# Moving every tile that TensorE reads to a multiple of 512 bytes in SBUF

## The chip, the cores and the metric

The kernel runs on one core of one Trainium2 chip. The metric is the device time of one execution in microseconds. Before the change the median of 3 runs is 1949.47 us (1949.44 to 1951.29).

## What is computed

One layer of a decoder: a gMLP token mixer and a SwiGLU feed-forward part, each followed by a residual and a layer norm, all in float32 on 2048 tokens of 1024 features.

```python
D_MODEL = 1024; SEQ = 2048; GM_CHUNK = 128; GM_GROUPS = 8; FFN_HIDDEN = 2816
mod = silu(c) @ mod_w + mod_b                    # six vectors: sh1, sc1, g1, sh2, sc2, g2
h = x * (1 + sc1) + sh1
u, v = split(gelu(h @ gm_w_in + gm_b_in))
v = layer_norm(v)                                # then 128x128 causal products, group by group
y = (u * (w_masked @ v + b_s)) @ gm_w_out
x = layer_norm(2 ** 0.25 * x + (1 + g1) * y)
h = x * (1 + sc2) + sh2
g, u = split(h @ ffn_w_in)
x = layer_norm(2 ** 0.25 * x + (1 + g2) * ((silu(g) * u) @ ffn_w_out))
```

## The kernel before

Every large product is carried as three products of `float32r` parts: an operand is split by `parts` (L88, L89) into a high part (a cast on ScalarE) and a low part (a subtraction on VectorE), and hi*hi, hi*lo and lo*hi are added up in PSUM. Such a tile (`UNIT`) holds 2 x 512 values of 4 bytes on each of 128 partitions, 4096 bytes a partition. One matmul reads a stationary operand of 128 values (512 bytes a partition, loaded just ahead of it) and a moving operand of 512 values (2048 bytes a partition). There are 7881 of these matmuls.

The mixer runs over 4 blocks of 512 tokens. In each, `token_major` (L192) makes v from `hT` and `wv`, `feature_major` (L209) makes u from `wu` and `hT`, small 128x128 products (L310) do the spatial gate, and `token_major` (L192 again) makes y from `yT` and `wo`. The feed-forward part takes Winograd's form of a 2x2 product, seven products P1 to P7. `ffn_in` (L428) runs over two halves of the tokens, 11 pairs of hidden tiles each, the seven products in the order P1, P2, P5, P6, P7, P4, P3, and gate and up ("g" and "u" in the names) for each; one such product is 12 matmuls. `ffn_out` (L577) takes the products in the order P2, P5, P3, P1, P6, P7, P4; in each step it runs 12 matmuls of the first half of the tokens and then 12 of the second; P4's second half comes last, by itself.

Tiles lie in pools that are stacked from the left end of SBUF upward or from the right end downward (`phase("left", ...)`, `phase("right", ...)`). At the left end come 16384 bytes of scratch for DMAs that GpSimd issues (there are two, L110 and L112), then constants and the small tiles of the norms, up to byte 20032, which is 64 modulo 512. At the right end the pools begin at byte 229344, which is 480 modulo 512. All slots of the large pools are whole multiples of 512 bytes, so that every large tile of the left begins at 64 modulo 512 and every one of the right at 480. The matmuls read them so (from the built program's addresses):

| matmuls | stationary operand | moving operand | count |
|---|---|---|---|
| v, L192 | `hT`, right, 480 | `wv`, left, 64 | 768 |
| u, L209 | `wu`, left, 64 | `hT`, right, 480 | 768 |
| y, L192 | `yT`, left, 64 | `wo`, left, 64 | 768 |
| P1 and P2 of `ffn_in`, L428 | weights, left, 64 | `A11`, `A12`, right, 480 | 1056 |
| the other five of `ffn_in`, L428 | weights, left, 64 | left, 64 | 2640 |
| `ffn_out` without P4, first half, L577 | `alw`, right, 480 | `wd_w`, right, 480 | 792 |
| `ffn_out` without P4, second half, L577 | `alw`, left, 64 | `wd_w`, right, 480 | 792 |
| P4 of `ffn_out`, L577 | `alw`, right (222) or left (75) | `wd_w`, left, 64 | 297 |

So in 3606 matmuls (768 + 768 + 1056 + 792 + 222) the two operands begin at different places modulo 512, and in 4275 at the same.

Of the kernel before, what the change touches and what calls it, by code (L numbers as in the profile page):

```python
# [24 lines left out]

# Winograd's form of the 2x2 product C = A B in seven products:
#   P1 = A11 B11   P2 = A12 B21   P5 = S1 T1   P6 = S2 T2   P3 = S4 B22   P7 = S3 T3   P4 = A22 T4
#   S1 = A21 + A22   S2 = S1 - A11   S3 = A11 - A21   S4 = A12 - S2
#   T1 = B12 - B11   T2 = B22 - T1   T3 = B22 - B12   T4 = B21 - T2
#   C11 = P1 + P2         C12 = P1 + P6 + P5 + P3  # L30
#   C21 = P1 + P6 + P7 + P4   C22 = P1 + P6 + P7 + P5
A_OF = {1: "A11", 2: "A12", 3: "S4", 4: "A22", 5: "S1", 6: "S2", 7: "S3"}
# [4 lines left out]
def gmlp_swiglu_layer(  # L37
# [6 lines left out]
):  # L44
    """One gMLP + SwiGLU layer.

    Every large product is float32 carried as three one-pass products: an operand is the exact
    sum of two float32r parts (12 significant bits each), hi and lo, and hi*hi + hi*lo + lo*hi
    is accumulated in float32. The products of the feed-forward part take Winograd's form.
    """  # L50
    nc = tc.nc
# [4 lines left out]
    dram = ctx.enter_context(tc.tile_pool(name="dram", bufs=1, space=bass.MemoryType.DRAM))  # L56

    ROW, HALF, UNIT = ([P, D], F32), ([P, 512], F32), ([P, 2, 512], F32R)
    cur, n = {}, [0]

    def phase(side, **tags):
        """Open one pool for each tag: tag=(number of slots, shape and type). Close what is returned."""
        st = ExitStack()
        for tag, (bufs, kind) in tags.items():
            n[0] += 1
            p = st.enter_context(tc.tile_pool(name=f"{tag}{n[0]}", bufs=bufs, side=side, reuse_waits="tile"))
            cur[tag] = (p, kind)
        return st
# [16 lines left out]
    def parts(src, name, tag):  # L85
        """[P, 512] float32 as its hi and lo parts."""
        o = new(tag, name, UNIT)
        nc.scalar.copy(out=o[:, 0, :], in_=src)  # L88
        nc.vector.tensor_tensor(out=o[:, 1, :], in0=src, in1=o[:, 0, :].bitcast(F32), op=ALU.subtract)  # L89
        return o  # L90
# [7 lines left out]

    # constants
    ident = const.tile([P, P], F32, name="ident")  # L100
# [5 lines left out]

    # conditioning: mod = silu(c) @ mod_w + mod_b, one column per 128 outputs
    modc = const.tile([P, 48], F32, name="modc")
# [29 lines left out]
    def spread(k, name):  # L138
        """Columns [P, 1] * ND as one row on every partition, by way of DRAM."""
        line = dram.tile([ND, P], F32, name=f"{name}_line")  # L140
        nc.sync.dma_start(out=line.rearrange("d p -> p d"), in_=modc[:, k * ND : (k + 1) * ND])
        t = new("late", name)
        nc.sync.dma_start(out=t, in_=line.rearrange("d p -> (d p)").partition_broadcast(P))
        return t
# [4 lines left out]
    def norm_of(st, name):  # L149
        """Mean and 1 / sqrt(var + EPS)."""  # L150
        mv = small.tile([P, 2], F32, tag="mv", name=f"{name}_mv")
        nc.vector.bn_aggr(out=mv, in_=st)
        ve = small.tile([P, 1], F32, tag="ve", name=f"{name}_ve")
        nc.vector.tensor_scalar(ve, mv[:, 1:2], EPS, None, ALU.add)  # L154
        rs = small.tile([P, 1], F32, tag="rs", name=f"{name}_rs")
        nc.gpsimd.tensor_tensor(out=rs, in0=ve, in1=mhalf, op=ALU.pow)  # L156
        # one Newton step: rs * (1.5 - 0.5 * ve * rs^2)
        nw = small.tile([P, 1], F32, tag="nw", name=f"{name}_nw")
        nc.vector.scalar_tensor_tensor(out=nw, in0=rs, scalar=ve, in1=rs, op0=ALU.mult, op1=ALU.mult)
        nc.vector.tensor_scalar(nw, nw, -0.5, 1.5, ALU.mult, ALU.add)  # L160
        nc.vector.tensor_tensor(out=rs, in0=rs, in1=nw, op=ALU.mult)
        return mv[:, 0:1], rs
# [10 lines left out]
    def ahead(makers, depth=2):  # L173
        """The makers' results in order; each is made `depth` uses before its own."""
        made = [m() for m in makers[:depth]]

        def results():
            for i in range(len(makers)):
                if i + depth < len(makers):
                    made.append(makers[i + depth]())  # L180
                yield made[i]

        return results()

    def token_major(operands, nk, name, between=()):
        """out[t, :] over NT token tiles: sum over k of a_k[:, t].T @ w_k, in all 8 banks."""
        ps = [[bank(f"{name}_ps{t}{h}") for h in range(2)] for t in range(NT)]
        for k, (a, w) in enumerate(operands):
            for t in range(NT):
                for part, wpart in HL:  # L190
                    for h in range(2):
                        nc.tensor.matmul(  # L192
                            ps[t][h],
                            lhsT=a[:, part, t * P : (t + 1) * P],
                            rhs=w[h][:, wpart, :],
                            start=(k == 0 and part == 0 and wpart == 0),
                            stop=(k == nk - 1 and part == 1),
                        )
            for f in between[k :: nk]:
                f()  # L200
        return ps

    def feature_major(w, rhs, name):
        """out[j, tokens] of 128 features: w is [d, (d-tile, j)] in parts."""
        ps = bank(name)
# [13 lines left out]
    x1d = [dram.tile([TB, D], F32, name=f"x1d{b}") for b in range(NB)]  # L219
    # left operands of the feed-forward products, [k, tokens of one half] in float32  # L220
    hop = [[[dram.tile([P, TB], F32, name=f"hop{o}_{k}_{sb}") for sb in range(2)] for k in range(NK)] for o in range(7)]
# [11 lines left out]
    def setup_spatial():  # L233
        # masked w_s, transposed to [s, (g, t)]
        wm = new("bcv", "wm")
# [5 lines left out]
        )  # L241
        # tb[c, (g, t)] = ln_b[c] * sum_s w[t, s] + b_s[g, t]
        lb = new("raw", "lnb_bc")
# [122 lines left out]
    def h2_part(b, i, cols_of, tag):  # L366
        """Transposed, modulated feature tiles i and NK + i; with the second half of a super-block their left operands.

        cols_of(t, q) is token tile t's columns of feature tile i + q * NK.
        """  # L370
        sb = b // 2
# [28 lines left out]
    def a_operands(r0, r1, name):  # L400
        """Raw [k0, (t0, t1)] and [k1, (t0, t1)] -> S1..S4 and the seven left operands in float32."""
        a11, a21, a12, a22 = r0[0], r0[1], r1[0], r1[1]
# [7 lines left out]
    def load_ops(sb, names):  # L410
        def tag_of(n, k):
            """A22, S3 and most of S4 take rows that the mixer leaves."""
            return "late" if n in ("A22", "S3") or (n == "S4" and k > 1) else "ops" + n

        out = {}
        for n in names:
            out[n] = []
            for k in range(NK):
                t = new("h3" if sb else "s" if n in ("S3", "A22") else "hr", f"h2{n}r_{sb}_{k}", HALF)
                nc.sync.dma_start(out=t, in_=hop[A_AT[n]][k][sb])  # L420
                out[n].append(parts(t, f"h2{n}_{sb}_{k}", tag_of(n, k)))
        return out

    def ffn_in(sb, ops, between={}):
# [12 lines left out]
        def weight(fp, pr, gu):  # L437
# [6 lines left out]
            b11, b12, b21, b22 = B[gu]  # L444
            # T1, T2 take the place of B11, T3 of B12, T4 of B21
            if pr == 5:
# [13 lines left out]
        for fp in range(NP):  # L460
            X, Y, Z, c1, u1, u2 = {}, {}, {}, {}, {}, {}
            for pr in order:
# [30 lines left out]
                if (fp, pr) in between:  # L493
                    between[fp, pr]()
            # C11 in c1, C12 in u1, C22 in u2, C21 in X
            for cc in (c1, u2, u1):
# [8 lines left out]
    def residual(b, t, r, cs, st, scaled=False):  # L505
        """r * (1 + g2) + alpha * x1 on half a row, with its sums."""
        xt = new("xr", f"xr{b}_{t}_{cs.start}")[:, : cs.stop - cs.start]
# [10 lines left out]
    def finish(b, t, r, st, e):  # L518
        """Norm and store of one token tile; `e` adds, or none where the wait for it would be the longest."""
        row = b * TB + t * P  # L520
# [15 lines left out]

    # token tile pairs: (sb, p) joins tile p of the first and of the second half of sb
    prs = [(sb, p) for sb in range(2) for p in range(NT)]
# [44 lines left out]
    def ffn_out():  # L583
# [29 lines left out]

        # P3 adds to P5 and P6, P7, P4 to P1 where they accumulate; the last product of the second half
        # comes pair by pair, so that each pair's norm follows at once
        steps = [(pr, k) for pr in (2, 5, 3, 1, 6, 7, 4) for k in range(NP)]
# [153 lines left out]
```

## Time and profile before

| | |
|---|---|
| median of 3 runs | 1949.47 us (1949.44 to 1951.29) |
| profiled execution, first to last instruction (its span) | 1948.5 us; the page gives no other time of it |
| median less span | 1.0 us |
| TensorE busy | 1875.5 us, 96% of the span, 8297 matmul records |
| VectorE, ScalarE, GpSimd busy | 1284.1, 760.2, 716.6 us |
| DMA | 312.77 MB, 161 GB/s on average |

Busy time of TensorE is modelled and overlaps from one matmul to the next, so the pace of the matmuls is not read from it. The pace is read from the chain of work that ended last: a piece "2.72 ... x12" says that 12 matmuls in a row took 2.72 us of that chain. The granted clock of TensorE (PEclk) is in shares of full speed: 1.00 is 2.4 GHz and 0.50 is 1.2 GHz.

### The profile page before, as it was taken

The page shows a single profiled execution, that of the slowest core. Times are in us where ns is not written, and L with a number is a line of the kernel's source. Part 1 is how long each engine was busy: PE and PEld are TensorE (multiplying, and loading weights), DVE is VectorE, ACT ScalarE, POOL GpSimd, SP SyncE. Part 2 cuts the span into 40 slices and gives each one's busy share as a digit, 9 for nine tenths or more (in the row PEclk, how much of TensorE's full clock was granted, in tenths as well). Part 3 has the DMA queues.
Part 4 walks back from the last instruction along what each step waited for, and adds up shares of the span by engine and source line. Part 5 has one row for each costly group of instructions (what it writes and reads, how often), then busy time and mean ns, then how long its engine had stood idle before and what let it go on. Part 6 is the DMA issues. An engine that isn't in the chain of part 4 may idle for free.

```text
span 1948.5 us, 23471 instructions
## 1 busy us (share of the span) xinstructions
PE 1875.5 (96%) x8297; PEld 1532.5 (79%) x8297; DVE 1284.1 (66%) x1855; ACT 760.2 (39%) x1251; POOL 716.6 (37%) x465
## 2 busy tenths in 40 slices
PE   7999999999999999999999999999999999999776
PEld 6787788778888788888887888888888888887655
DVE  8486866786758856555668566556554433476998
ACT  3432552543545434333345333333343443332321
POOL 0000500550402666645544554355431200244834
PEclk9999999999999999999999999999999999999978
DMA  9358546464455444542236323322347644555542
GB/s 355 121 184 304 170 153 229 156 226 155 141 184 184 140 157 152 173 142 97 103 117 195 121 102 106 108 91 103 113 145 246 215 130 140 168 172 172 191 151 108
DMA packets 135064, 312.77 MB, mean 161 GB/s; under 512 B 16641, under 2 KB 21025, under 8 KB 134946
## 3 DMA queue, kind: packets, MB, share of 16 engines
q1 hardware_dynamic: 134882, 311.24, 47.2%
q8 instruction: 65, 1.06, 0.2%
q14 instruction: 53, 0.43, 0.1%
q0 software_dynamic: 64, 0.03, 0.0%
HBM read 239.37 MB, written 71.84 MB: 160 GB/s over the span
## 4 chain that ended last, share of the span: by engine, by line
PE 80%; DVE 11%; DMA 4%; issue 2%; POOL 1%; ACT 1%; SPq 0%; DVEq 0%; POOLq 0%; ACTq 0%
PE o L577 18%; PE v_ps L192 8%; PE u_ps L209 7%; PE y_ps L192 6%; PE f_4u_X L428 1%; PE f_2u_X L428 1%; PE f_5u_X L428 1%; PE f_3u_X L428 1%; PE f_8u_X L428 1%; PE f_7u_X L428 1%; PE f_6u_X L428 1%; PE f_8g_X L428 1%; PE f_7g_X L428 1%; PE f_6g_X L428 1%; PE f_3g_X L428 1%
## 5 line engine op out<-in xcount | busy, mean ns | idle before, releaser
L577 PE MATMUL o<-wd_w,alw 128*128 128x512 f32 (+1 forms) x1881 | 434.4, 393 | 33.3 <-DVE o L77 28.2
L577 PEld LDWEIGHTS o<-wd_w,alw 128*128 128x128 f32 x1881 | 352.8, 191 | 114.8 <-ACT alw L88 23.5
L192 PE MATMUL v_ps<-wv,hT 128*128 128x512 f32 x768 | 184.8, 402 | 16.7 <-ACT wv L88 11.8
L89 DVE TENSOR_TENSOR alw<-al,alw 128x512 fp32r<-128x512 f32 x154 | 130.1, 877 | 98.0 <-ACT alw L88 97.8
L192 PEld LDWEIGHTS v_ps<-wv,hT 128*128 128x128 f32 x768 | 147.1, 192 | 53.5 <-ACT wv L88 12.1
L209 PE MATMUL u_ps<-hT,wu 128*128 128x512 f32 x768 | 186.5, 402 | 1.8 <-DVE v L281 1.3
L192 PE MATMUL y_ps<-wo,yT 128*128 128x512 f32 x768 | 175.7, 390 | 1.9 <-DVE sv L315 1.9
L209 PEld LDWEIGHTS u_ps<-hT,wu 128*128 128x128 f32 x768 | 144.9, 191 | 36.9 <-issue 1.9
L192 PEld LDWEIGHTS y_ps<-wo,yT 128*128 128x128 f32 x768 | 143.7, 188 | 32.3 <-issue 1.8
L156 POOL TENSOR_TENSOR ln_rs<-ln_ve,mhalf 128x1 f32<-128x1 f32 x32 | 27.8, 876 | 361.2 <-DVE ln_ve L154 349.9
L88 ACT CAST alw<-al 128x512 fp32r<-128x512 f32 x154 | 88.8, 618 | 149.2 <-PE o L577 121.6
L89 DVE TENSOR_TENSOR wu<-wu_raw,wu 128x512 fp32r<-128x512 f32 x64 | 65.8, 1042 | 53.6 <-ACT wu L88 53.5
L80 POOL TENSOR_TENSOR chain<-wd,chain 128x512 f32<-128x512 f32 x22 | 33.7, 1532 | 159.4 <-DVE wd_w L89 127.2
L88 ACT CAST wv<-wv_raw 128x512 fp32r<-128x512 f32 x64 | 37.5, 619 | 106.0 <-PE v_ps L192 43.2
L118 DVE SCALAR_TENSOR_TENSOR modw<-modw,cact 128x1024 f32<-128x1024 f32 x48 | 58.3, 1217 | 19.9 <-DMA modw<-in_modwT 19.9
L89 DVE TENSOR_TENSOR wv<-wv_raw,wv 128x512 fp32r<-128x512 f32 x64 | 47.4, 759 | 22.4 <-ACT wv L88 22.2
L89 DVE TENSOR_TENSOR wo<-wo_raw,wo 128x512 fp32r<-128x512 f32 x64 | 46.4, 732 | 20.4 <-ACT wo L88 20.2
L89 DVE TENSOR_TENSOR wd_w<-wd,wd_w 128x512 fp32r<-128x512 f32 x44 | 34.8, 791 | 37.0 <-ACT wd_w L88 37.0
L88 ACT CAST wo<-wo_raw 128x512 fp32r<-128x512 f32 x64 | 38.6, 616 | 43.5 <-PE y_ps L192 42.1
L88 ACT CAST wu<-wu_raw 128x512 fp32r<-128x512 f32 x64 | 38.2, 616 | 36.1 <-PE v_ps L192 20.8
L88 ACT CAST wd_w<-wd 128x512 fp32r<-128x512 f32 x44 | 27.2, 619 | 48.1 <-PE o L577 36.0
L359 POOL TENSOR_TENSOR r<-r,ln1g_bc 128x1024 f32<-128x1024 f32 x16 | 41.5, 2611 | 11.5 <-ACT r L168 11.5
(604 smaller groups left out, 3879.7 us busy)
## 6 DMA issues: line engine op xcount, KB each, us to landing
al<-aop SPq DMA_DIRECT2D x154, 256.0 KB, 3.2
wd<-in_wd SPq DMA_DIRECT2D x99, 256.0 KB, 3.2
modw<-in_modwT SPq DMA_DIRECT2D x48, 512.0 KB, 8.4
aop<-aop_s SPq DMA_DIRECT2D x88, 256.0 KB, 2.0
wv_raw<-in_wv SPq DMA_DIRECT2D x32, 512.0 KB, 4.6
wu_raw<-in_wu SPq DMA_DIRECT2D x32, 512.0 KB, 4.3
wo_raw<-in_wo SPq DMA_DIRECT2D x32, 512.0 KB, 3.5
hop<-h SPq DMA_DIRECT2D x40, 256.0 KB, 3.1
```

Source lines behind the costliest of these rows:

```text
L80: nc.gpsimd.tensor_tensor(out=o, in0=a, in1=b, op=ALU.subtract)
L88: nc.scalar.copy(out=o[:, 0, :], in_=src)
L89: nc.vector.tensor_tensor(out=o[:, 1, :], in0=src, in1=o[:, 0, :].bitcast(F32), op=ALU.subtract)
L118: nc.vector.scalar_tensor_tensor(out=w, in0=w, scalar=1.0, in1=env["cact"], op0=ALU.mult, op1=ALU.mult, accum_out=modc[:, j : j + 1],)
L156: nc.gpsimd.tensor_tensor(out=rs, in0=ve, in1=mhalf, op=ALU.pow)
L192: nc.tensor.matmul(ps[t][h], lhsT=a[:, part, t * P : (t + 1) * P], rhs=w[h][:, wpart, :], start=(k == 0 and part == 0 and wpart == 0), sto ...
L209: nc.tensor.matmul(ps, lhsT=w[d // 4][:, wpart, (d % 4) * P : (d % 4 + 1) * P], rhs=rhs[d][:, part, :], start=(n == 0), stop=(n == 3 * ND ...
L359: nc.gpsimd.tensor_tensor(out=r, in0=r, in1=env["ln1g"], op=ALU.mult)
L428: nc.tensor.matmul(ps, lhsT=w[:, wpart, k * P : (k + 1) * P], rhs=a[k][:, part, :], start=(first and k == 0 and wpart == 0 and part == 0), ...
L577: nc.tensor.matmul(ps[:, cs], lhsT=a[:, part, p * P : (p + 1) * P], rhs=w[:, wpart, cs], start=(first and part == 0 and wpart == 0), stop= ...
```

## The change

Two pools are opened ahead of all the large ones, one on the left of 448 bytes a partition and one on the right of 480 bytes, and their tiles are set to zero once. The scratch of GpSimd's DMAs is 4096 bytes in place of 16384. Comments and docstrings go as well (not shown).

```diff
+    for side, pad in (("left", 448), ("right", 480)):
+        pads = ctx.enter_context(tc.tile_pool(name=f"pad_{side}", bufs=1, side=side))
+        nc.vector.memset(pads.tile([P, pad // 4], F32, name=f"pad_{side}"), 0.0)
+
     ROW, HALF, UNIT = ([P, D], F32), ([P, 512], F32), ([P, 2, 512], F32R)
...
-    nc = bacc.Bacc("TRN2", target_bir_lowering=False, num_devices=1)
+    nc = bacc.Bacc("TRN2", target_bir_lowering=False, num_devices=1, dynamic_dma_scratch_size=4096)
```

In the built program the left pools now begin at byte 8192 and the right ones at 228864, both 0 modulo 512. Every large tile of the left has moved down by 11840 bytes and every one of the right by 480; each kept its slot among the others. In all 7881 matmuls of the table both operands now begin at 0 modulo 512. Two constants did not come to a multiple of 512: the identity of the transposes (L382) and `ones`, which both remain at 128 modulo 512.

On every engine the instructions stand in the same order as before, with the same operands, but for two on VectorE. At the start of the program VectorE had these rows (line, operation, tile written, tiles read, elements):

```order
L766 UNCONDITIONAL_BRANCH
L103 MEMSET ones 128x128
L118 SCALAR_TENSOR_TENSOR modw_321,modc<-modw_321,cact 128x1024
L122 TENSOR_SCALAR modc<-modc,modbc 128x1
L118 SCALAR_TENSOR_TENSOR modw_325,modc<-modw_325,cact 128x1024
L122 TENSOR_SCALAR modc<-modc,modbc 128x1
```

And it has these in the changed kernel, where line numbers from here on are 5 higher:

```order
L771 UNCONDITIONAL_BRANCH
L61 MEMSET pad_left 128x112
L61 MEMSET pad_right 128x120
L108 MEMSET ones 128x128
L123 SCALAR_TENSOR_TENSOR modw_331,modc<-modw_331,cact 128x1024
L127 TENSOR_SCALAR modc<-modc,modbc 128x1
```

Two small memsets now stand ahead of the one that was there; nothing else has moved on any engine.

## Rows read from the trace of the kernel before

**Rows 1.** The page: span, busy time, and the chain that ended last.

```profile
span 1948.5 us, 23471 instructions
...
PE 1875.5 (96%) x8297; PEld 1532.5 (79%) x8297; DVE 1284.1 (66%) x1855; ACT 760.2 (39%) x1251; POOL 716.6 (37%) x465
...
PE 80%; DVE 11%; DMA 4%; issue 2%; POOL 1%; ACT 1%; SPq 0%; DVEq 0%; POOLq 0%; ACTq 0%
```

**Rows 2.** Chain, 820 to 846 us, `ffn_in`: start us, us, what.

```profile
821.45 2.82 PE f_5u_Y L428 x12
824.26 2.72 PE f_5g_Z L428 x12
826.99 2.72 PE f_5u_Z L428 x12
829.71 2.72 PE f_5g_X L428 x12
```

**Rows 3.** Chain, whole span and two stretches of the mixer.

```profile
267.77 5.63 PE u_ps L209 x24
274.29 43.55 PE y_ps L192 x192
465.86 44.80 PE v_ps L192 x192
```

**Rows 4.** Chain, two neighbouring stretches of one step of `ffn_out`, and its longest piece.

```profile
1554.10 2.96 PE o L577 x13
...
1556.83 3.04 PE o L577 x13
...
1477.81 293.32 PE o L577 x1270
```

**Rows 5.** Chain, 65.6 to 69.7 and 66.2 to 69.0 us; then the first stretch's granted clock.

```profile
65.59 4.14 PE u_ps L209 x9
...
65.59 3.71 PE u_ps L209 x8
...
65.60:69.70 4.10, 4.10 (x10) 3.23 (x11) 4.10 (x10) 2.80 (x5) 0.00 (x0) 0.50 0.68 253
```

**Rows 6.** Chain, 1127 to 1165 us, `ffn_in`, second half.

```profile
1135.85 2.75 PE f_2g_Z L428 x12
1138.60 2.72 PE f_2u_Z L428 x12
```

**Rows 7.** Stretches: length, then PE, PEld, DVE, ACT, POOL busy (count), PEclk, DMA share, GB/s.

```profile
180.00:223.00 43.00, 42.70 (x172) 34.24 (x173) 42.35 (x94) 17.35 (x24) 14.82 (x9) 0.93 0.60 208
...
657.00:1030.00 373.00, 370.58 (x1626) 303.78 (x1626) 230.01 (x249) 147.03 (x251) 205.53 (x132) 1.00 0.41 140
...
1478.00:1772.00 294.00, 294.00 (x1275) 239.25 (x1274) 141.87 (x191) 108.71 (x189) 55.80 (x38) 1.00 0.55 177
1772.00:1840.00 68.00, 64.86 (x281) 52.18 (x280) 60.43 (x93) 19.36 (x28) 48.94 (x32) 1.00 0.57 186
1840.00:1866.00 26.00, 1.34 (x4) 0.42 (x2) 24.89 (x24) 14.46 (x25) 15.19 (x9) 0.60 0.72 245
```

**Rows 8.** Chain: pieces in which VectorE makes weights for u or adds up `ffn_out`.

```profile
222.92 2.88 DVE wu L89
228.33 3.25 DVE wu L89 x2
...
354.74 2.85 DVE wu L89 x2
...
1814.41 2.89 DVE alw L89
```

**Rows 9.** Groups: ScalarE's casts of weights, of `hT` and of `alw`.

```profile
L88 ACT CAST alw<-al 128x512 fp32r<-128x512 f32 x154 | 88.8, 618 | 149.2 <-PE o L577 121.6
...
L88 ACT CAST wo<-wo_raw 128x512 fp32r<-128x512 f32 x64 | 38.6, 616 | 43.5 <-PE y_ps L192 42.1
...
L88 ACT CAST hT<-xT 128x512 fp32r<-128x512 f32 x32 | 19.3, 619 | 17.2 <-DVE xT L265 17.0
```

**Rows 10.** VectorE in order of time, 0 to 12 us.

```profile
0.91 0.17 DVE L103 MEMSET ones<- 128x128 f32 x1 [0.91 <-PEq L760]
6.77 1.23 DVE L118 SCALAR_TENSOR_TENSOR modw<-modw,cact 128x1024 f32<-128x1024 f32 x1 [5.70 <-DMA modw<-in_modwT]
```

**Rows 11.** The page: the queue of GpSimd's DMAs.

```profile
q0 software_dynamic: 64, 0.03, 0.0%
```

## The prediction

> **What bounds the kernel now.** I read the page first: TensorE is busy for 96% of the span and carries 80% of the chain that ended last; VectorE has 11% of the chain and DMA 4% [rows 1]. So most of the time is a row of matmuls, and the question is what sets their pace. I read it from pieces of the chain in which nothing but matmuls stands, since a busy share says nothing of pace.
>
> In `ffn_in` twelve matmuls of P2 (`f_5u_Y`) took 2.82 us and twelve of the next products 2.72 us [rows 2]. Instructions, shapes and parts are the same; what differs is the place of the moving operand: `A12` lies on the right (480 modulo 512), that of the others on the left (64), as all the weights do. Per matmul this is 2.82 / 12 = 235 ns against 2.72 / 12 = 226.7 ns. The mixer says the same [rows 3]: y, with both operands on the left, ran at 43.55 / 192 = 226.8 ns; v, with its stationary operand on the right and the moving one on the left, at 44.80 / 192 = 233.3 ns; u, the other way round, at 5.63 / 24 = 234.6 ns. In `ffn_out` I cut one step in two [rows 4]: thirteen matmuls with both operands on the right took 2.96 us, thirteen with the stationary one on the left 3.04 us. The right is not slow by itself, then. Both at 64 and both at 480 give the low pace, one at each gives the high one, whichever operand it is. What costs is that the two places differ.
>
> A second reading says that it is a matter of reading SBUF. Where the granted clock was 0.50 (1.2 GHz), eight matmuls of u with the same unlike operands took 3.71 us and nine 4.14 [rows 5]: 0.43 us for one, which is 512 columns at 1.2 GHz and no more (512 / 1.2 = 426.7 ns). At 2.4 GHz 512 columns are 213.3 ns; the like pairs are 13.4 ns above that and the unlike pairs 20 to 21.
>
> **The change part by part.** It makes all 7881 pairs like. The value I take for a pair at 0 and 0 is the 226.7 ns that like pairs have at 64 and at 480. The trace shows none at 0, so its bounds are the 213.3 ns of the columns alone and the 235 ns of the worst rows; 226.7 is the nearest, since it held at two places that have nothing else in common.
>
> Gain if every nanosecond counted:
> - v: 768 x (233.3 - 226.8) = 5.0 us.
> - u: 768 x (234.6 - 226.8) = 6.0 us.
> - P1 and P2 of `ffn_in`: 88 groups of twelve x (2.82 - 2.72) = 8.8 us; some of the 88 groups read 2.81, which makes it 7.9; I take 8.3.
> - `ffn_out`: the piece of 1270 matmuls ran at 293.32 / 1270 = 231.0 ns [rows 4], half of it unlike pairs, so these stood 2 x (231.0 - 226.7) = 8.6 ns higher; the cut step gives (3.04 - 2.96) / 13 = 6.2. With 7 ns, 1014 x 7 = 7.1 us (6.3 to 8.7).
>
> Together 26.4 us.
>
> What of it is not on the path:
> - In v of the second block VectorE was busy for 42.35 of 43.00 us [rows 7]; a faster TensorE waits for it. 192 x 6.5 ns = 1.2 us lost.
> - Where u begins in the second and third block the chain runs through VectorE's weights for u [rows 8]. I take half of the gain of u in these two blocks as lost: 0.5 x 2 x 192 x 7.8 ns = 1.5 us.
> - From 1772 to 1866 us the chain runs through VectorE too (60.43 of 68.00 us busy, then 24.89 of 26.00 us with TensorE at a stand) [rows 7, 8]. The 132 matmuls of P4's first half lie there: 132 x 7 ns = 0.9 us lost.
> - `ffn_in` and the first six products of `ffn_out` lose nothing: VectorE was busy for 230.01 of 373.00 us and 141.87 of 294.00, so it has room for a pace 3% higher [rows 7].
> - Like pairs do not all run at 226.7: one group of S1 took 2.75 us beside 2.72 with the same kinds of operands at other addresses [rows 6]. If one in four of the 3606 / 12 = 300 groups that become like comes out so, that is 75 x 0.03 = 2.3 us.
>
> That leaves 26.4 - 1.2 - 1.5 - 0.9 - 2.3 = 20.5 us.
>
> The rest costs nothing. The two memsets are smaller than the one of 0.17 us beside them and stand where VectorE then waited 5.70 us for a DMA [rows 10]; without that cover they would cost under 0.4 us. The smaller scratch concerns 64 packets of 0.03 MB [rows 11] at the start; were it too small, the first user of `modbc` (L122) would wait longer than it does now behind those 5.70 us. The other engines' tiles move too, but their times do not follow the place: ScalarE's cast took 616 ns from left to left (`wo`), 619 where `hT` is written on the right, and 618 for `alw`, mostly read from the right [rows 9]. DMA rows now begin on a multiple of 512; the trace has no such row, DMA has 4% of the chain (78 us) [rows 1], and I take nothing, with a few us of gain as the far end. [...]
>
> The sum against the profiled execution is 1948.5 - 20.5 = 1928.0 us of span; the median of the runs stands 1.0 us above that span, so 1929 us.
>
> [...] The rows show 2.82 against 2.72 us for the same twelve matmuls [rows 2]. [...]
>
> **The rivals.**
> - *A lower pace at 0 than at 64 or 480.* If starting on a 512-byte boundary also removes part of the 13.4 ns that like pairs still pay, all 7881 matmuls gain: 105 us at most (7881 x 13.4 ns), so 1929 - 105 = 1824 us, and 1887 with two fifths of it. For it: the 13.4 ns vanish at the low clock [rows 5], so something about the reads can be better. Against it: 64 and 480 differ in every alignment from 64 bytes up and give the same pace [rows 3, 4].
> - *No change.* The unlike places are not the cause, or the pace gained is taken back by VectorE, which has 11% of the chain [rows 1]. Then 1949.5, within 0.2% (3.9 us), which is about what a measurement of this kernel can tell from no change. Against it: the matmuls of all five stages fall in line by place alone [rows 2 to 4]. [...]
> - *Slower.* If 0 and 0 is the place where reads of the two operands meet most often, the 4275 pairs that were like lose their low pace. The price is 4275 x 8 ns = 34 us at the pace of the worst rows, while the unlike pairs gain nothing: 1984 us. The change turns into a loss as soon as a pair at 0 and 0 costs over 3.3 ns more than one at 64 and 64 (7881 x 3.3 ns is the gain of 26 us). For it: 2.75 beside 2.72 [rows 6] shows that addresses matter beyond the place modulo 512. Against it: that step is only 2.5 ns a matmul.
>
> **How the numbers follow.** My forecast (pairs at 0 run at about 226.7 ns) has a chance of 0.63, the lower pace 0.13, no change 0.15, slower 0.09. The predicted time is that of the forecast, 1929 us. Its own range is 1921 (nothing lost, and the upper value for `ffn_out`: 28 us) to 1938 (twice the losses, and 4 ns a matmul in `ffn_out`: 26.4 - 11.8 - 3.1 = 11.5 us). For 8 in 10 I add no change and the upper part of the lower pace: 1890 to 1951. Faster by over 0.2% takes the forecast and the lower pace, 0.76; within 0.2%, 0.15; slower, 0.09.
>
> **What would show it.** Right: the pieces of v, u, P1 and P2 read 5.44 us for 24 and 2.72 for 12, those of y and of P5 stay at 43.5 and 2.72, and the piece of `ffn_out` runs at 227 to 228 ns a matmul; VectorE's and ScalarE's means stay. Wrong: y and P5 move too (either rival on the pace at 0), v and u keep 233 ns and more (the place is not the cause), or the pieces are faster and the gaps at 180 to 240 and 1772 to 1866 us grow by as much.

## The result and the profile after

The changed kernel takes 1928.6 us (median of 4 runs, 1926.23 to 1932.37) against 1949.45 us before: a ratio of 0.9892, 95% interval 0.9872 to 0.9912, 20.9 us faster. The forecast was 1929 us. The profiled execution took 1927.45 us and has a span of 1925.7, that is 22.8 us less than the profiled one of before.

From the page of the changed kernel: the span, the busy time, and the chain that ended last. They answer to [rows 1]; lines of the kernel are 5 higher now.

```profile
span 1925.7 us, 23473 instructions
...
PE 1850.6 (96%) x8297; PEld 1532.6 (80%) x8297; DVE 1271.0 (66%) x1857; ACT 760.3 (39%) x1251; POOL 725.6 (38%) x465
...
PE 78%; DVE 13%; DMA 5%; issue 2%; POOL 1%; ACT 1%; SPq 0%; DVEq 0%; POOLq 0%; ACTq 0%
```

VectorE's and ScalarE's busy time hardly moved (1271.0 us against 1284.1, 760.3 against 760.2), and the same 8297 matmul records are busy for 25 us less. Where that comes from stands in the chain. The pieces that answer to [rows 2 to 4] and [rows 6] (start us, us, what):

```profile
460.76 43.52 PE v_ps L197 x192
...
529.63 5.46 PE u_ps L214 x24
...
558.59 43.32 PE y_ps L197 x191
...
808.39 2.74 PE f_5g_Y L433 x12
811.12 2.72 PE f_5u_Y L433 x12
813.84 2.72 PE f_5g_Z L433 x12
...
1121.50 2.72 PE f_2g_Z L433 x12
1124.22 2.72 PE f_2u_Z L433 x12
...
1459.91 287.88 PE o L582 x1270
```

v runs at 43.52 / 192 = 226.7 ns a matmul (233.3 before), u at 5.46 / 24 = 227.5 (234.6), P2 at 2.72 to 2.74 us for twelve (2.82), the long piece of `ffn_out` at 287.88 / 1270 = 226.7 ns (231.0). y stays at 43.32 / 191 = 226.8. One thing moved that was not meant to: the group of S1 (`f_2g_Z`, of P5) that read 2.75 us in [rows 6] reads 2.72.

### The profile page after: what moved, and what is told of

Same layout as the page of the kernel before. It is cut to its first block, busy times and chain, and to the rows that moved or that the text cites. A ratio compares the mean times of both kernels' runs of the same rounds, so it can differ in the third digit from the quotient of the medians.

```text
span 1925.7 us, 23473 instructions
## 1 busy us (share of the span) xinstructions
PE 1850.6 (96%) x8297; PEld 1532.6 (80%) x8297; DVE 1271.0 (66%) x1857; ACT 760.3 (39%) x1251; POOL 725.6 (38%) x465
## 4 chain that ended last, share of the span: by engine, by line
PE 78%; DVE 13%; DMA 5%; issue 2%; POOL 1%; ACT 1%; SPq 0%; DVEq 0%; POOLq 0%; ACTq 0%
PE o L582 17%; PE u_ps L214 7%; PE y_ps L197 6%; PE v_ps L197 5%; DVE modw L123 2%; PE f_5u_X L433 1%; PE f_4u_X L433 1%; PE f_3u_X L433 1%; PE f_2u_X L433 1%; PE f_9u_X L433 1%; PE f_9g_X L433 1%; PE f_8u_X L433 1%; PE f_8g_X L433 1%; PE f_7u_X L433 1%; PE f_7g_X L433 1%
## 5 line engine op out<-in xcount | busy, mean ns | idle before, releaser
L582 PE MATMUL o<-wd_w,alw 128*128 128x512 f32 (+1 forms) x1881 | 427.9, 390 | 34.9 <-DVE o L82 29.5
L197 PE MATMUL v_ps<-wv,hT 128*128 128x512 f32 x768 | 179.5, 396 | 16.0 <-ACT wv L93 11.9
L197 PEld LDWEIGHTS v_ps<-wv,hT 128*128 128x128 f32 x768 | 146.5, 191 | 48.1 <-ACT wv L93 12.1
L214 PE MATMUL u_ps<-hT,wu 128*128 128x512 f32 x768 | 181.9, 396 | 0.7 <-ACT h L388 0.5
L94 DVE TENSOR_TENSOR wu<-wu_raw,wu 128x512 fp32r<-128x512 f32 x64 | 59.5, 946 | 50.5 <-ACT wu L93 50.1
```

The costliest lines, as they stand in the source:

```text
L197: nc.tensor.matmul(ps[t][h], lhsT=a[:, part, t * P : (t + 1) * P], rhs=w[h][:, wpart, :], start=(k == 0 and part == 0 and wpart == 0), sto ...
L214: nc.tensor.matmul(ps, lhsT=w[d // 4][:, wpart, (d % 4) * P : (d % 4 + 1) * P], rhs=rhs[d][:, part, :], start=(n == 0), stop=(n == 3 * ND ...
L582: nc.tensor.matmul(ps[:, cs], lhsT=a[:, part, p * P : (p + 1) * P], rhs=w[:, wpart, cs], start=(first and part == 0 and wpart == 0), stop= ...
```

## Experiments

**One side alone.** The kernel before with a pad on the right only, so that all operands begin at 64 modulo 512, and the scratch as it was.

```diff
+    for side, pad in (("right", 416),):
+        pads = ctx.enter_context(tc.tile_pool(name=f"pad_{side}", bufs=1, side=side))
+        nc.vector.memset(pads.tile([P, pad // 4], F32, name=f"pad_{side}"), 0.0)
```

> One pad of 416 bytes on the right, none on the left, scratch of 16384 bytes as before: every matmul reads both operands at 64 modulo 512. Theory (only the distance between the two operands modulo 512 counts): v, u, P1 and P2 and the second half of a step of ffn_out all at 226.7 to 227.5 ns, as y had at 64 and 64 before; time 1929 us, at most 2 us more for the slow minority that like pairs had at 64. Rival (0 modulo 512 is what counts): v 233 and u 234.6 ns as before, 2.81 us for twelve of P1 and P2, time 1949 us.

It took 1932.35 us, ratio 0.9916 (0.9898 to 0.9933). The chain of this kernel:

```profile
465.46 43.52 PE v_ps L197 x192
...
534.32 5.46 PE u_ps L214 x24
...
1124.15 2.72 PE f_2u_Y L433 x12
1126.87 2.72 PE f_2g_Z L433 x12
...
1465.28 287.88 PE o L582 x1270
```

Every pace is that of the changed kernel, with no large tile at a multiple of 512 or 256. So the place itself does not set the pace; the distance of the two operands does. The tiles of the left lie here exactly where they lay before, and still the group of S1 went from 2.75 us [rows 6] to 2.72. It was no matter of its addresses, then. It runs right behind P2, which was unlike before and is like now: an unlike product (its operands at different places) slows the first like one behind it a little. The starts of the single matmuls in the trace of the kernel before show how far that reaches: in the P5 groups behind P2 (both halves together) the first five of the twelve matmuls follow each other at 228.6 to 233.5 ns on average, and from the seventh on at 226.6 to 227.1.

**The scratch alone.** The other part of the change without the pads.

```diff
-    nc = bacc.Bacc("TRN2", target_bir_lowering=False, num_devices=1)
+    nc = bacc.Bacc("TRN2", target_bir_lowering=False, num_devices=1, dynamic_dma_scratch_size=4096)
```

> The scratch of 4096 bytes alone: the left end is still at 64 modulo 512, the right at 480. Theory (place of the operands is all): 1949 us within 4 us, v 233 and u 234.6 ns. Rival (the scratch itself, or the constants' new place, gives part of the gain): 1930 to 1945 us with the paces unchanged.

It took 1951.26 us, ratio 1.0009 (0.9997 to 1.0021), with the paces of before: its longest piece of `ffn_out` took 293.32 us again, its v 44.80 us. The scratch gives nothing and costs nothing that can be told.

**How far apart is apart.** Two versions of the changed kernel with the right side moved off again, by a small pool ahead of the first pool of each group there.

```diff
         st = ExitStack()
+        apart = {"hT": 256, "opsA11": 256, "ld": 256}.get(next(iter(tags))) if side == "right" else None
+        if apart:
+            n[0] += 1
+            q = st.enter_context(tc.tile_pool(name=f"apart{n[0]}", bufs=1, side=side))
+            nc.vector.memset(q.tile([P, apart // 4], F32, name=f"apart{n[0]}"), 0.0)
```

> The changed kernel with 256 bytes more on the right ahead of each group of pools there: left at 0, right at 256 modulo 512. Theory (512 is the period, any distance within it costs): v, u, P1 and P2 at 233 to 236 ns, about 1949 us. Rival A (the period is 256 or less): 226.7 ns and 1928 us. Rival B (operands that are far apart meet less often): under 226.7 ns, under 1925 us.

```diff
-        apart = {"hT": 256, "opsA11": 256, "ld": 256}.get(next(iter(tags))) if side == "right" else None
+        apart = {"hT": 32, "opsA11": 64, "ld": 128}.get(next(iter(tags))) if side == "right" else None
```

> The changed kernel with the right moved by 32 bytes in the mixer (v, u), by 64 in ffn_in (P1, P2) and by 128 in ffn_out (second half of a step, P4). Theory (period 512): all three at 232 to 236 ns. Rival (period 64): u and v at 233 to 235, P1 and P2 2.72 us for twelve and ffn_out 226.7. Rival (period 128): only ffn_out at 226.7 ns. Time between 1929 and 1949 us accordingly, since v and u hold some 11 us of the gain, P1 and P2 8 and ffn_out 7.

The first took 1925.98 us (one run), the second 1944.5 (one run). The chain of the first, 256 bytes apart:

```profile
459.79 43.52 PE v_ps L202 x192
...
528.67 5.46 PE u_ps L219 x24
...
810.90 2.72 PE f_5u_Y L438 x12
...
1461.69 287.88 PE o L587 x1270
```

And of the second, where u is 32, P2 64 and `ffn_out` 128 bytes apart:

```profile
534.94 5.60 PE u_ps L219 x24
...
700.70 2.80 PE f_2u_Y L438 x12
...
1473.77 293.71 PE o L587 x1270
```

At 256 everything has the low pace, so my theory's period of 512 was wrong. At 32 u takes 5.60 / 24 = 233.3 ns, at 64 P2 takes 2.80 / 12 = 233.3, and at 128 `ffn_out` is as slow as before (293.71 against 293.32 us). The rivals' periods of 64 and 128 fall as well. What counts is whether the two operands begin at the same place modulo 256. Each of these distances was tried in one stage only, and none finer than 32 bytes.

**The cost nearly doubled.** The changed kernel with the pool of prepared weights of the mixer and of `ffn_in` moved by 96 bytes, and what follows it put back, so that products that were like before the change become unlike too.

```diff
+    def gap(st, side, size):
+        n[0] += 1
+        q = st.enter_context(tc.tile_pool(name=f"gap{n[0]}", bufs=1, side=side))
+        nc.vector.memset(q.tile([P, size // 4], F32, name=f"gap{n[0]}"), 0.0)
...
         for tag, (bufs, kind) in tags.items():
+            if side == "left" and tag == "w":
+                gap(st, side, 96)
             n[0] += 1
...
             cur[tag] = (p, kind)
+            if side == "left" and tag == "w":
+                gap(st, side, 416)
```

> The changed kernel with the pool of prepared weights of the mixer and of ffn_in moved by 96 bytes (and what follows it put back to 0 by 416 bytes more): in v, u, y and all of ffn_in one operand is at 96 and the other at 0, 6000 unlike pairs where the first kernel had 3606; ffn_out stays like. Theory (the distance modulo 256 costs 6.5 to 8 ns a matmul): y and all products of ffn_in go to 233 to 235 ns (2.80 to 2.82 us for twelve, 44.8 for y's 192), the time to 1928.6 + 6000 x 7 = 1971 us, 1963 to 1973. Rival (the places of right and left tiles count, not the distance): y and P5 stay at 226.7 and the time at 1929 to 1935 us.

It took 1976.47 us, ratio 1.0152 (1.0135 to 1.0169): 48 us over the changed kernel where I expected 35 to 45, so a little past the theory's end and far from the rival. The chain:

```profile
271.23 44.82 PE y_ps L206 x192
...
465.13 44.80 PE v_ps L206 x192
...
1154.91 2.81 PE f_2u_Y L442 x12
1157.72 2.81 PE f_2g_Z L442 x12
...
1507.30 287.88 PE o L591 x1270
```

y and P5, which no kernel up to here slowed but for the first matmuls of P5 behind P2, now take 44.82 / 192 = 233.4 ns and 2.81 us; `ffn_out`, left like, keeps its 226.7. The pace by itself accounts for some 43 us (6000 matmuls at 7.2 ns more on average). Where `ffn_in` begins (600 to 720 us) TensorE also waited 11.9 us for operands in this kernel, against 4.3 in the changed one, so the theory's end was passed rather by waits than by a higher price of a matmul.

**Which load is in the way.** The low part of `yT` was put 128 bytes further from its high part, so that one third of y's matmuls have unlike operands among like ones.

```diff
-        o = new(tag, name, UNIT)
+        if tag == "yT":
+            o = new(tag, name).rearrange("p (a b) -> p a b", b=544)[:, :, 0:512]
+        else:
+            o = new(tag, name, UNIT)
...
-            env["mix"] = phase("left", yT=(8, UNIT), raw=(3, ROW), bcv=(3, ROW), vrow=(4, ROW))
+            env["mix"] = phase("left", yT=(8, ([P, 1088], F32R)), raw=(3, ROW), bcv=(3, ROW), vrow=(4, ROW))
```

> The changed kernel with the low part of yT 128 bytes further from its high part, so that in y the stationary operand is at 0 modulo 256 for two thirds of the 768 matmuls and at 128 for one third, while the moving operand stays at 0. Theory (a matmul is slowed by the load of the next one's weights, which goes on while it runs): slow, at 231 to 235 ns, are those whose successor reads the low part, and those that read the low part themselves but are followed by the high part run at 226.7. Rival (a matmul is slowed by its own weights' place): the other way round. Either way y's 192 take some 44.0 us in place of 43.5, and the time stays at 1926 to 1932 us.

Theory and rival both missed, and the run told neither from the other. From the chain:

```profile
559.56 44.42 PE y_ps L200 x191
```

This is 232.6 ns a matmul on average where both had 44.0 us for 192, and nearly the pace of matmuls that are all unlike, though two thirds of them are like; the granted clock was 1.00. By the starts in the trace, the mean step to the next matmul is 233.8, 231.2, 230.1, 232.0, 235.1 and 233.1 ns over the six of a group, of which the first four are like and the last two read the low part. So the unlike matmuls slow the like ones between them, as P2 did with P5, only here every group of six is mixed. Which load or read is in the way stays open. The time was 1946.59 us (one run), and most of that is a side effect: the larger tiles of `yT` changed which old tiles the pools of `ffn_in` lie over, and TensorE waited 13.9 us in place of 4.3 where `ffn_in` begins (4.5 us for `f_0u_w` alone). The paces from there on are those of the changed kernel.

**What like pairs still pay.** In y, the product of the high part of `yT` with the low part of the weights loads and uses 64 columns in place of 128; half of this correction is left out.

```diff
+                        m = 64 if name[0] == "y" and wpart else P
                         nc.tensor.matmul(
-                            ps[t][h],
-                            lhsT=a[:, part, t * P : (t + 1) * P],
+                            ps[t][h][0:m, :],
+                            lhsT=a[:, part, t * P : t * P + m],
```

> The changed kernel; in y, the matmuls of the high part of yT with the low part of the weights load and use 64 of the 128 columns of the stationary operand (half of this correction is left out, a third of y's matmuls). Theory (the 13.4 ns above 213.3 that like pairs still pay is the read of the next weights, in proportion to its bytes): a matmul whose successor loads 64 columns takes about 220 ns, the others 226.7. Rival (the 13.4 ns are a fixed step from one matmul to the next): all stay at 226.7. The time falls by at most 256 x 7 ns = 2 us.

It took 1930.59 us (one run). From the chain:

```profile
560.01 43.95 PE y_ps L198 x191
```

y did not get faster but slower, 230 ns a matmul against 226.8. By the starts in the trace the mean steps over the six of a group lie between 228.3 and 232.0 ns, none near the 220 of the theory. So the 13.4 ns above 213.3 (an estimate: half of the 426.7 ns that a matmul took at a granted clock of 0.50 before) do not shrink with the columns that are loaded. The rival (all stay at 226.7) does not hold either. Why y became slower, and what the 13.4 ns are, stays open.

**Where gain was given back.** In the third block of the mixer TensorE now waits longer for VectorE ahead of y. From the waits of the kernel before, and then of the changed one (us in total, times, longest):

```profile
PE y_ps L192 <- DVE sv L315: 1.9, 2, 1.4
```

```profile
PE y_ps L197 <- DVE sv L320: 3.9, 1, 3.9
```

VectorE has eight modulations of g2 on top in this block; they were put into the fourth.

```diff
-        elif b == 2:
+        elif b == 3:
             mods = [mod_of(g2, 5, d, 1.0) for d in range(ND)]
```

> The changed kernel with the eight modulation columns of g2 made in the fourth block in place of the third; they are needed in ffn_out only. Theory (part of the gain is given back in the third block because VectorE, with these eight on top, delivers sv and yT late and y starts 4 us late): the stall ahead of y in that block shrinks from 4 us to under 1 and the time falls from 1928.6 to 1922 to 1926 us. Rival (the fourth block, or the free rows of the pool late, is as tight): the stall moves, 1927 to 1931 us.

It took 1927.85 us, ratio 0.9901 (0.9887 to 0.9916): the wait fell to 2.2 us, and the total did not move by anything that can be told from the changed kernel's 0.9892 (0.9872 to 0.9912). The theory's 1922 to 1926 us is missed by 2 us; the eight modulations are a part of that wait and not all of it.

**The smallest pad.** If the distance modulo 256 is all, 160 bytes on the right do it (left at 64, right at 320 modulo 512), without the left pad and without the smaller scratch.

```diff
+    for side, pad in (("right", 160),):
+        pads = ctx.enter_context(tc.tile_pool(name=f"pad_{side}", bufs=1, side=side))
+        nc.vector.memset(pads.tile([P, pad // 4], F32, name=f"pad_{side}"), 0.0)
```

> The kernel before with one pad of 160 bytes on the right and nothing else: left at 64, right at 320 modulo 512, that is both at 64 modulo 256; scratch of 16384 bytes. Theory (the distance modulo 256 is all that counts): every matmul kind at 226.7 to 227.3 ns, time equal to the changed kernel's beside it within 0.2%, 1927 to 1933 us. Rival (starting at a multiple of 256 or 512 gives something more, to DMAs or to VectorE): the changed kernel is 3 us or more faster than this one.

> The changed kernel once more, on the same chip as the pad of 160 bytes. Both theories: 1928 us within 4 us; it is there to be compared with.

The pad of 160 bytes took 1933.52 us, ratio 0.9929 (0.9914 to 0.9944); the changed kernel beside it 1930.48, ratio 0.9909 (0.9896 to 0.9921). The paces are the same to the last digit: this kernel's v, u and `ffn_out`, in the chain:

```profile
465.19 43.52 PE v_ps L197 x192
...
534.07 5.46 PE u_ps L214 x24
...
1465.09 287.88 PE o L582 x1270
```

The medians differ by 3.0 us, the intervals overlap, and the pad of 416 bytes lay at 1932.35 too. Part of it in the profiled executions is TensorE's granted clock behind two waits. Stretches of the pad of 160 bytes, then of the changed kernel beside it (length, PE, PEld, DVE, ACT, POOL busy, PEclk, DMA share, GB/s):

```profile
236.00:248.00 12.00, 8.94 (x35) 6.94 (x34) 2.62 (x4) 10.71 (x16) 0.00 (x0) 0.72 0.67 252
...
415.00:431.00 16.00, 11.96 (x42) 9.32 (x41) 14.18 (x20) 6.89 (x12) 4.24 (x3) 0.79 0.58 194
```

```profile
236.00:248.00 12.00, 8.99 (x48) 7.40 (x46) 2.33 (x4) 11.71 (x17) 0.00 (x0) 0.86 0.68 259
...
415.00:431.00 16.00, 11.87 (x45) 9.29 (x45) 14.16 (x19) 6.89 (x12) 4.52 (x3) 0.89 0.55 190
```

In the first kernel the lower clock lasted longer at both places. By the starts of the matmuls it lost 1.5 us on the other kernel at the first place and 0.8 at the second, and 1.9 more in the first half of P4, at a mean clock of 0.88 against 0.93 (1847 to 1890 us); it had been 1.8 us ahead. The 3.0 us lie within the 0.2% of the theory and also meet the 3 us of the rival, so the run does not decide between them beyond the pace. Whether starting at a multiple of 256 has anything to do with the clock, or chance has, is not settled. By the outer bounds of the two intervals such a gain is at most (0.9944 - 0.9896) x 1949 = 9 us, and it may be nothing.

## Why the prediction was right

**The mechanism.** The step "what costs is that the two places differ" held: the pad on one side shows that like pairs are fast at 64, the run with the weights 96 bytes off that y and P5 become slow as soon as their operands differ: y went from 226.8 to 233.4 ns a matmul by the place of its moving operand `wo` alone, P5 from 2.72 to 2.81 us for twelve. The value taken for a pair at 0 and 0, 226.7 ns, is what was measured. Why a difference of places costs time is not shown by any run; the prediction's "a matter of reading SBUF" rests on the low clock alone, where an unlike pair took 0.43 us [rows 5]. The profile gives that clock only as a share. By the starts in the trace of before, matmuls with 512 columns followed each other at 426.7 ns where it was 0.50, and those with 256 at 213.3, that is at 1.2 columns a ns; the prediction's 2.4 GHz and its 213.3 ns for 512 columns are twice that pace, an estimate for 1.00 that no matmul of 512 columns in the two traces reached.

**The terms.** Forecast for v, u, P1 and P2, and `ffn_out`: 5.0, 6.0, 8.3 and 7.1 us. By the pieces after: v 768 x (233.3 - 226.7) = 5.1; u 768 x (234.6 - 227.5) = 5.5; P1 and P2 88 groups, each 0.08 to 0.10 us, so 7.0 to 8.8; the long piece of `ffn_out` 293.32 - 287.88 = 5.4 for 1270 of its 1881 matmuls, so some 8.0 for all. Together about 26.5 us, as forecast (26.4).

**The losses.** The sum of 5.9 us is near what was given back (26.5 - 22.8 = 3.7 us in the profiled executions, 5.6 by the medians), but its terms were in good part wrong, so that the sum came out near is partly luck. The starts of pieces of the chain show how much earlier the changed kernel reached a place:

| piece of the chain | before, us | after, us | earlier by |
|---|---|---|---|
| u, first block, a group of 24 | 105.15 | 102.09 | 3.1 |
| y, second block | 274.29 | 269.72 | 4.6 |
| v, fourth block | 465.86 | 460.76 | 5.1 |
| y, fourth block | 566.29 | 558.59 | 7.7 |
| `ffn_in`, first half, `f_2u_X` | 696.85 | 687.87 | 9.0 |
| `ffn_in`, second half, `f_2u_X` | 1127.42 | 1113.34 | 14.1 |
| `ffn_out`, long piece | 1477.81 | 1459.91 | 17.9 |
| `ffn_out`, the last product (P4) | 1866.42 | 1845.33 | 21.1 |

- A block should bring 11 / 4 = 2.8 us. The first and the fourth (5.1 to 7.7 up to its y) do; the second and third together bring 2.0 in place of 5.5 from the first group of 24 to v of the fourth block. So some 3.5 us were lost in the two middle blocks, where I had 1.2 + 1.5. The amount was a little small, and both places were off. By the starts of the single matmuls, v of the second block, where I had 1.2 us lost, brought 2.8 (3.4 us earlier at its first matmul, 6.2 at its last); its length does not follow the pace of its matmuls (52.6 us before, 49.8 in the changed kernel, 48.1 in the one with its weights 96 bytes off). The first four groups of u behind it, where I had the weights for u, kept their gain (6.7 us earlier at the fourth). The loss came behind them: 2.7 us up to the sixth group, with a wait of 3.0 us for ScalarE's `u` ahead of the last transposes (`h2T_ps`; 1.3 before) and a mean clock of 0.79 from 239 to 246 us behind it, where it had been 1.00 before. In the third block 3.2 us went in y, behind its wait for `sv` (8.3 us earlier at its first matmul, 5.1 at its last).
- "2.3 us because like pairs do not all run at 226.7" was wrong in sign. The 2.75 us of [rows 6] was no matter of addresses but came from the unlike P2 ahead, and it went away with it.
- Around P4 I had 0.9 us, and took 1772 to 1866 us for the place of its first half. By the count of matmuls (264 for each of the six products ahead of P4) that stretch is P7; P4 begins at its end. The long piece gained 5.4, and by P4 the kernel was only 21.1 - 17.9 = 3.2 us further ahead, so 2.2 were lost from 1751 to 1845 us, where VectorE is busy for 82.75 of 94.00 us and the mean clock was 0.84, against 0.89 from 1772 to 1866 us before. The first half of P4 itself lost nothing: it brought 1.5 us (21.1 earlier at its first matmul, 22.6 behind its last).

What I had not put into the sum is the clock. Behind some of the waits for VectorE the granted clock was 0.50 for a while (in the third block from 419.5 to 422.7 us, behind a wait of 3.9 us for `sv`), and matmuls then took some 427 ns each. The changed kernel's stretch there:

```profile
411.00:423.00 12.00, 8.13 (x32) 6.30 (x31) 11.49 (x16) 5.75 (x10) 4.76 (x3) 0.86 0.65 219
```

VectorE is busy for 11.49 of the 12.00 us, TensorE stands for almost four, and its mean granted clock there is 0.86; at the same place before (420 to 430 us) it stayed 1.00. Over the whole execution the mean went from 0.985 to 0.983. Counted from the starts, 36 matmuls before and 48 after took some 427 ns, at the low clock, so up to 12 x 0.2 = 2.4 of the 3.7 us given back may be the clock. But the kernel with the small scratch alone, at the paces of before, had 52 of them in its profiled execution, so that the change brings more of them is not shown.

**What cost nothing.** VectorE at the start of the changed kernel (start us, us, instruction, what it had waited for):

```profile
0.91 0.15 DVE L61 MEMSET pad_left<- 128x112 f32 x1 [0.91 <-PEq L765]
1.03 0.16 DVE L61 MEMSET pad_right<- 128x120 f32 x1
1.16 0.17 DVE L108 MEMSET ones<- 128x128 f32 x1
6.64 1.23 DVE L123 SCALAR_TENSOR_TENSOR modw<-modw,cact 128x1024 f32<-128x1024 f32 x1 [5.32 <-DMA modw<-in_modwT]
```

The two memsets took 0.15 and 0.16 us and came off the wait behind them, which is 5.32 us in place of 5.70 [rows 10]. ScalarE's casts of 128x512 take 616 to 623 ns, before 616 to 622. DMA, for which I took nothing, shows nothing that follows the place: weights for the modulations (512 KB) landed after 8.4 us before and 8.1 in the changed kernel, but after 8.1 with the left at 64 modulo 512 and the pad of 416 bytes, and after 8.4 with the left at 64 and the pad of 160.

## What to carry to other kernels

Look at the pace of matmuls of one shape by where their two operands lie; if it differs between stages, compare the starting places of stationary and moving operand before looking for anything else. In this kernel, float32r with 512 columns at a granted clock of 1.00, it was enough that they agree modulo 256 bytes: 160 bytes of pad on one side gave all of the matmuls' pace (v at 226.7 ns in place of 233.3). Other types and widths were not tried. Unlike matmuls slowed the like ones among them (y ran at 232.6 ns on average with one third unlike), so a stage is worth repairing as a whole; and a TensorE that was faster by 3% in these stages gave part of its gain back, partly in waits for the engines that feed it (3.7 of 26.5 us in the profiled execution).

## What the runs showed of the hardware

- A float32r matmul of 128x128 by 512 columns, in a row of the same kind at a granted clock of 1.00, took 226.7 ns (u 227.5) where the two operands began at the same place modulo 256 bytes (at 0 and 0, 64 and 64, 0 and 256, 64 and 320), and 233 to 235 ns at distances of 32, 64 and 96. At 128 the piece of `ffn_out`, half of it unlike pairs, ran at 231.3 ns, as before at 96 (231.0). At a granted clock of 0.50 the unlike pair took 0.43 us [rows 5], and the like pairs of the changed kernel took as long (426.7 ns on average, 7 matmuls of v and 7 of y).
- The slow pace reached beyond the unlike pairs: in y, two thirds like pairs among one third unlike ones took 232.6 ns on average, and in `ffn_in` a like product right behind an unlike one took 2.75 us in place of 2.72, nearly all of it in its first five matmuls (228.6 to 233.5 ns, from the seventh on 226.6 to 227.1).
- Loading 64 columns in place of 128 for a third of the matmuls made the stage slower (230 ns against 226.8), not faster.
